# Eight of the 22 up-projection steps as seven block products, with weight sums made by adding transfers in a hybrid SSD, attention and ConvFFN layer

## The chip, the cores and the metric

The kernel runs on one core of one Trainium2 chip. A core has five engines that work side by side: TensorE (PE; its weight loads are listed as PEld), VectorE (DVE), ScalarE (ACT), GpSimd (POOL) and SyncE (SP), which here only issues transfers. Each engine has its own in-order queue and waits on semaphores; transfers (DMAs) run on 16 DMA engines. The metric is device microseconds of the whole program, as the median of several runs.

## The reference, cut to what matters

One diffusion layer over 512 latent tokens with 256 context tokens, D_MODEL = 1024, all in fp32. An input projection feeds two mixers (a bidirectional state-space scan and windowed attention); their merged output is added to x; then comes the gated ConvFFN, which is what the change is about:

```python
D_FF = 2816
def conv_ffn(h, w_up, conv_w, conv_b, w_down):
    u = dwconv_centred(h @ w_up, conv_w, conv_b)      # (512, 5632), 3 taps along the tokens
    a, b = u[..., :D_FF], u[..., D_FF:]
    return (jax.nn.silu(a) * b) @ w_down
...
x = x + gt2 * conv_ffn(modulate(x, norm2_g[l], sh2, sc2), w_up[l], ffn_conv_w[l], ffn_conv_b[l], w_down[l])
```

## The kernel before

**Products.** Every fp32 operand of a large product is split into a high part, its value rounded to fp32r, and a low part, the rest. `gemm` then issues three TensorE products for each block of 128 input channels: high weight by high input, high weight by low input, low weight by high input. The split of a weight is a ScalarE copy (the cast, `whi`) and a VectorE subtraction (`wlo`); `load` issues the transfer on SP's queue into one of three `raw` buffers and emits both. `run` goes through a list of steps; each names the weights it needs, and the next one is loaded and split one key ahead. Outside blocks marked as manual, a scheduler orders the instructions of each engine ahead of time, by its own estimate of when each is ready and by the order of the program; inside `manual_schedule` the order on the named engines is the written one.

**Attention.** A planner (`Plan`) writes out the order of the attention blocks and of 30 projections beside them (`BESIDE`, numbered g). Behind each of their weight splits (`low`, L1112), `sum_step` puts one or two transfers on POOL's queue: sums of blocks of the down projection's weight, made in DRAM. Each sum is a plain copy and then a transfer with `accum_op=ALU.add` onto it. 32 such transfers are issued here, the last behind split g = 23. The down projection already runs as seven products of blocks instead of eight (Strassen and Winograd's scheme) with them.

**The scan.** Its first group's x blocks are turned by VectorE in blocks of 32 and go out to `xs_d` and back in by transfers on POOL's queue (`blocks_out` and `blocks_in`, L1473 and L1482); VectorE weighs what came back (`xw`, L1590), and TensorE forms the states from that (L1621).

**Up projection.** 22 steps (`up_step(t)`, t = 0 to 21). Each multiplies two weights of 1024 by 128 channels, `("up", t)` for a and `("up", 22 + t)` for b, with the normed input (`h2h`, `h2l`, in the trace mh and ml): 8 blocks of k, three products each, 512 tokens wide, into two PSUM banks. Then the three taps (`conv`: one ScalarE instruction, L2058, two VectorE ones, L2059 and L2060), SiLU of a (L2066) and a times b (L2072) into `F["x"]`. After each step `f_sums(t)` works on that step's 256-column halves: sums and splits for the down projection (L2039 to L2052), six VectorE instructions for two steps. Step 0 runs in halves of 256 tokens because the norm (`norm2_k`, L2021 to L2028) only then delivers its input.

Woven between the up steps stand the last eight steps of the modulation (`m_step(24)` to `(31)`, L811 and L813, whose results go through a chain of transfers on POOL, `fold`), eight `x1_turn` (a VectorE transpose of a block of x1 into a `te` buffer, L2120, and four transfers to DRAM on SP's queue), `x1_rows` and `row_tiles`. The small buffers have tags: `te` and `tc` have two each, `ta` three, `tm` one.

Names in the trace: tile `wraw` is a weight as loaded, `whi` and `wlo` its two parts, `dsum` a sum of down weights in DRAM, `x_d` x1 in DRAM.

## Time and profile before

| | |
|---|---|
| Median of 3 runs | 1214.62 us (1214.22 to 1214.86) |
| The profiled execution | 1214.44 us |
| Its span in the trace | 1212.7 us |
| TensorE busy | 1204.0 us, 99% of the span, 6429 products |
| VectorE, ScalarE, POOL busy | 917.3, 684.6, 265.6 us |
| Up projection | from 859 us to 1101 us after the span's start |

The span runs from the first instruction recorded to the end of the last; the execution's own time has 1.7 us around it. Busy shares are means over stages that have different limits. The views used below: the page (busy times, the chain of work that ended last), busy times by stretch, groups of instructions by line and shape (busy time, mean duration in ns, idle time before), rows of single instructions in order of time (start, duration), and transfers by line (median time from issue to landing).

### The profile page before, as it was taken

The page shows a single profiled execution, that of the slowest core. Times are in us where ns is not written, and L with a number is a line of the kernel's source. Part 1 is how long each engine was busy: PE and PEld are TensorE (multiplying, and loading weights), DVE is VectorE, ACT ScalarE, POOL GpSimd, SP SyncE. Part 2 cuts the span into 40 slices and gives each one's busy share as a digit, 9 for nine tenths or more (in the row PEclk, how much of TensorE's full clock was granted, in tenths as well). Part 3 has the DMA queues.
Part 4 walks back from the last instruction along what each step waited for, and adds up shares of the span by engine and source line. Part 5 has one row for each costly group of instructions (what it writes and reads, how often), then busy time and mean ns, then how long its engine had stood idle before and what let it go on. Part 6 is the DMA issues. An engine that isn't in the chain of part 4 may idle for free.

```text
span 1212.7 us, 17847 instructions
## 1 busy us (share of the span) xinstructions
PE 1204.0 (99%) x6429; PEld 1006.4 (83%) x6429; DVE 917.3 (76%) x1476; ACT 684.6 (56%) x1269; POOL 265.6 (22%) x274
## 2 busy tenths in 40 slices
PE   9999999999999999999999999999999999999998
PEld 6798888888878878788787888888988888888886
DVE  5857887888565588788887977677677777668787
ACT  4657887778543457476575674223544343436654
POOL 0000121100102546265382780000200100110021
PEclk9999999999999999999999999999999999999999
DMA  9655789844747736567467568677265634436652
GB/s 368 257 144 185 161 232 269 169 136 137 170 153 228 229 106 197 162 161 189 147 175 265 178 232 267 223 251 236 53 163 146 200 113 139 130 106 225 213 186 97
DMA packets 129417, 224.30 MB, mean 185 GB/s; under 512 B 27336, under 2 KB 70640, under 8 KB 129328
## 3 DMA queue, kind: packets, MB, share of 16 engines
q1 hardware_dynamic: 115248, 195.61, 51.5%
q0 software_dynamic: 13792, 27.27, 10.0%
q8 instruction: 51, 0.84, 0.3%
q14 instruction: 38, 0.31, 0.1%
q10 hardware_dynamic: 288, 0.27, 0.1%
HBM read 196.17 MB, written 45.02 MB: 199 GB/s over the span
## 4 chain that ended last, share of the span: by engine, by line
PE 93%; DMA 2%; DVE 1%; POOL 1%; issue 1%; ACT 1%; DVEq 0%; POOLq 0%; ACTq 0%
PE acc L238 18%; PE acc L241 18%; PE acc L239 18%; PE score L979 3%; PE po L1028 3%; PE pt L1015 2%; PE mis L582 2%; PE mis L1759 2%; PE mis L1602 2%; DMA xs_d<-xb 2%; PE mis L2310 2%; PE mis L2311 2%; PE mis L2309 2%; PE mis L1767 1%; PE acc L2310 1%; PE acc L2311 1%
## 5 line engine op out<-in xcount | busy, mean ns | idle before, releaser
L184 DVE TENSOR_TENSOR wlo<-wraw,whi 128x1024 fp32r<-128x1024 f32 (+1 forms) x115 | 148.3, 1289 | 87.9 <-ACT whi L183 84.7
L183 ACT CAST whi<-wraw 128x1024 fp32r<-128x1024 f32 (+1 forms) x115 | 120.3, 1047 | 154.0 <-PE acc L239 104.6
L238 PE MATMUL acc<-hlh,whi 128*128 128x512 f32 x472 | 192.8, 409 | 0.0
L241 PE MATMUL acc<-hlh,wlo 128*128 128x512 f32 x472 | 185.6, 393 | 0.0
L239 PE MATMUL acc<-hll,whi 128*128 128x512 f32 x472 | 185.0, 392 | 0.0
L238 PE MATMUL acc<-mh,whi 128*128 128x512 f32 x368 | 143.3, 389 | 0.0
L239 PE MATMUL acc<-ml,whi 128*128 128x512 f32 x368 | 143.2, 389 | 0.0
L241 PE MATMUL acc<-mh,wlo 128*128 128x512 f32 x368 | 143.2, 389 | 0.0
L241 PEld LDWEIGHTS acc<-hlh,wlo 128*128 128x128 f32 x472 | 88.6, 188 | 19.9 <-issue 0.5
L238 PEld LDWEIGHTS acc<-hlh,whi 128*128 128x128 f32 x472 | 88.8, 188 | 17.6 <-issue 2.8
L239 PEld LDWEIGHTS acc<-hll,whi 128*128 128x128 f32 x472 | 88.9, 188 | 17.4 <-issue 2.2
L241 PEld LDWEIGHTS acc<-mh,wlo 128*128 128x128 f32 x368 | 69.1, 188 | 14.4
L239 PEld LDWEIGHTS acc<-ml,whi 128*128 128x128 f32 x368 | 69.1, 188 | 14.3
L238 PEld LDWEIGHTS acc<-mh,whi 128*128 128x128 f32 x368 | 69.1, 188 | 14.2
L164 POOL DMA_DIRECT2D dsum<-wdn x24 | 25.3, 1119 | 194.4 <-DVE wlo L1112 183.7
L988 DVE CUSTOM_DVE_ANT_0 p<-score,winm,nsink 128x512 f32<-128x512 f32 (+1 forms) x64 | 51.9, 810 | 15.3 <-PE score L979 13.8
L995 ACT ACTIVATE p<-p,mneg 128x512 f32<-128x512 f32 (+1 forms) x64 | 49.8, 778 | 15.4 <-DVE mneg L988 14.8
L813 DVE SCALAR_TENSOR_TENSOR tm<-wraw,csil,tm 128x512 f32<-128x512 f32 x56 | 45.8, 818 | 12.2 <-DMA wraw<-wm 11.4
L1023 DVE TENSOR_TENSOR ptl<-pt,pth 128x512 fp32r<-128x512 f32 x72 | 47.5, 686 | 8.5 <-ACT pth L1019 7.7
L238 PE MATMUL acc<-hch,whi 128*128 128x256 f32 x176 | 53.2, 302 | 0.0
L1112 DVE TENSOR_TENSOR wlo<-wraw,whi 128x1024 fp32r<-128x1024 f32 x30 | 36.7, 1223 | 18.3 <-ACT whi L1109 18.0
L241 PE MATMUL acc<-hch,wlo 128*128 128x256 f32 x176 | 49.8, 283 | 0.0
(458 smaller groups left out, 3056.9 us busy)
## 6 DMA issues: line engine op xcount, KB each, us to landing
wraw<-wup SPq DMA_DIRECT2D x44, 512.0 KB, 3.9
dsum<-wdn POOLq DMA_DIRECT2D x24, 704.0 KB, 8.5
wraw<-wm SPq DMA_DIRECT2D x32, 512.0 KB, 4.2
fb<-cs_d SPq DMA_DIRECT2D x32, 512.0 KB, 7.1
wraw<-wx SPq DMA_DIRECT2D x24, 512.0 KB, 4.1
wm<-wm SPq DMA_DIRECT2D x16, 512.0 KB, 8.3
wraw<-wz SPq DMA_DIRECT2D x16, 512.0 KB, 5.0
far<-us_d SPq DMA_DIRECT2D x32, 256.0 KB, 5.3
```

Of the source, the lines that this page charges most:

```text
L183: F["cast"] = S.copy(hi[:, :n], r[:, :n])
L184: F["sub"] = V.tensor_tensor(lo[:, :n], r[:, :n], raw(hi[:, :n]), ALU.subtract)
L238: T.matmul(ps, wh, xh[:, k0 + k, :], start=a, stop=False)
L239: T.matmul(ps, wh, xl[:, k0 + k, :], start=False, stop=False)
L241: T.matmul(ps, wl, xh[:, k0 + k, :], start=False, stop=b)
L813: V.scalar_tensor_tensor(acc, r[:, u * 512 : u * 512 + 512], sc, acc, ALU.mult, ALU.add)
L979: T.matmul(ps[:, o : o + len(z) * P], Q[h][:, b * P : (b + 1) * P], k[:, j, z[0] * P : (z[-1] + 1) * P], start=v == 0 and o % 512 in (0, P ...
L988: V.tensor_tensor_reduce(p[:, :w], d["ps"][i][:, o0 : o0 + w], m, op0=ALU.add, op1=ALU.min, scale=1.0, scalar=nsink[:, h : h + 1], accum_o ...
L995: S.activation(p, p, AF.Exp, bias=d["mneg"][:, i : i + 1], scale=-1.0, accum_out=d["den"][:, i : i + 1])
L1023: V.tensor_tensor(d["ptl"][x], d["pt"][x], raw(d["pth"][x]), ALU.subtract)
L1028: T.matmul(d["po"], vst[:, cols[x], j, :], d[y][x], start=x == 0 and y == "pth", stop=x == c - 1 and y == "ptl")
L1112: sum_step(V.tensor_tensor(d["w"][1], d["r"], raw(d["w"][0]), ALU.subtract), 1 + (4 <= g < 12))
```

## The change

**Up steps 5 to 12 as seven products.** For these eight t the 2 by 2 block matrix of weights (a and b, each in two halves of k) and the 2 by 2 block matrix of inputs (halves of k, halves of the tokens) are multiplied with seven block products instead of eight. A block product (`seven(t, j)`) is 4 blocks of k, three products each, 256 tokens wide. It needs sums of weight blocks, sums of input blocks, and additions of the products.

- *Weight sums.* For each pair of steps four sums are made in DRAM (`US`), each by a copy and an adding transfer on POOL's queue: 32 transfers more, after the 32 of the down projection. `sum_step` now issues 1 behind splits g < 4, 2 behind g = 4 to 11, and 3 from g = 12 on. The steps load them (`us`, `u4`, `ul`), beside a's own weight (`ur`).
- *Input sums.* `input_sums` behind step 0 (six VectorE instructions of 1024 elements), `input_split` behind steps 1 and 2 (four casts and four subtractions).
- *The steps.* `seven_step(t)` writes out the order of TensorE, VectorE, ScalarE and POOL. Products 7 and 4 of a step run in the next one; quarters of the result are put together from two PSUM banks and a copy kept in a `te` buffer; taps read from SBUF; a times b moves to POOL (`put_up`). `seven_in(5)` splits the first weights behind step 4; `seven_out(13)` is up step 13 with the last two products of step 12 in it.
- *The rest.* `f_sums` runs in batches of two pairs of steps behind steps 14 to 21 and no longer after each step. `x1_turn` is kept in program order: 0 to 3 behind steps 1 to 3, 4 to 7 behind every second seven-product step. One modulation step follows each of steps 0 to 3, the last four come in steps 14 to 17.

```diff
+    SEVEN = range(5, 13)
+    US = [dpool.tile([len(SEVEN), P, 1024], F32, name="usum%d" % i) for i in range(2)]
+    for i in range(0, len(SEVEN), 2):
+        wa, wb = (wup[o + SEVEN[i] : o + SEVEN[i] + 2] for o in (0, NFF))
+        s, lo, hi = slice(i, i + 2), slice(0, 512), slice(512, 1024)
+        one, two, three, four = (u[s, :, z] for u, z in ((US[0], lo), (US[0], hi), (US[1], lo), (US[1], hi)))
+        for o, first_, more in (
+            (one, wb[:, :, lo], wb[:, :, hi]), (two, one, wa[:, :, lo]),
+            (three, wa[:, :, lo], wb[:, :, lo]), (four, two, wa[:, :, hi]),
+        ):
+            SUMS += [(o, first_, {}), (o, more, dict(accum_op=ALU.add, max_dma_last_dim=512))]
...
-            sum_step(V.tensor_tensor(d["w"][1], d["r"], raw(d["w"][0]), ALU.subtract), 1 + (4 <= g < 12))
+            sum_step(V.tensor_tensor(d["w"][1], d["r"], raw(d["w"][0]), ALU.subtract), 1 if g < 4 else 2 if g < 12 else 3)
...
+    def f_sums(p0, p1, pool=False):
+        x, y = F["x"]
+        z = slice(p0, p1)
+        e, f, g, h = (a[:, z, q] for a in (x, y) for q in HALF)
+        W = G if pool else V
+        f_split(0, z, e)
+        W.tensor_tensor(e, e, f, ALU.subtract)
+        f_split(1, z, e)
+        W.tensor_tensor(f, h, f, ALU.subtract)
+        V.scalar_tensor_tensor(e, e, -1.0, h, ALU.mult, ALU.subtract)
+        V.scalar_tensor_tensor(F["t"][:, z, :], e, -1.0, g, ALU.mult, ALU.subtract)
...
+    def input_sums():
+        r = F["h2"]
+        for k in (slice(0, HK, 2), slice(HK, KT, 2)):
+            V.tensor_tensor(r[:, k, :], raw(h2h[:, k, :]), raw(h2l[:, k, :]), ALU.add)
+        b11, b12, b21, b22 = (r[:, HK * i : HK * i + HK, z] for i in range(2) for z in HALF)
+        V.tensor_tensor(b11, b11, b12, ALU.subtract)
+        V.tensor_tensor(b12, b22, b12, ALU.subtract)
+        V.scalar_tensor_tensor(b22, b11, -1.0, b22, ALU.mult, ALU.subtract)
+        V.scalar_tensor_tensor(b21, b22, -1.0, b21, ALU.mult, ALU.subtract)
+        F["four"] = b11, b22, b12, b21
...
+    def seven(t, j):
...
+        for k in range(HK):
+            wh, wl = (x[:, k * P : k * P + P] for x in w)
+            st, en = k == 0 and j in (1, 2, 5), k == HK - 1 and j in (2, 3, 4)
+            T.matmul(ps[:, :HL], wh, of(0, k), start=st, stop=False, skip_group_check=True)
+            T.matmul(ps[:, :HL], wh, of(1, k), start=False, stop=False, skip_group_check=True)
+            T.matmul(ps[:, :HL], wl, of(0, k), start=False, stop=en, skip_group_check=True)
...
+    def put_up(t):
+        G.tensor_tensor(F["x"][t % 2][:, t // 2, :], B["oa", t], B["ob", t], ALU.mult)
...
+    def seven_step(t):
+        n, a, b = t + 1, t - 1, t - 2
...
+            with tc.manual_schedule(engines=EVERY):
+                if old:
+                    quarter(a, 12)
+                seven(t, 5)
+                if new:
+                    sum_cast("us", n)
+                if older:
+                    conv_rest("b", b, NFF + b)
+                    put_up(b)
+                if old:
+                    conv_first("a", a, a, "tb")
+                kept_half(t, 0, B["y", t])
+                if new:
+                    sum_low("us", n)
+                seven(t, 1)
+                if new:
+                    whole_cast(n)
+                kept_half(t, 1, B["x", t])
+                if old:
+                    conv_rest("a", a, a)
+                    seven(a, 7)
+                if new:
+                    sum_cast("u4", n)
+                sum_cast("ul", t)
+                if old:
+                    quarter(a, 22)
+                if new:
+                    whole_low(n)
+                if old:
+                    silu_a(a)
+                seven(t, 2)
+                quarter(t, 11)
+                if new:
+                    sum_low("u4", n)
+                sum_low("ul", t)
+                seven(t, 3)
+                quarter(t, 3)
+                if old:
+                    seven(a, 4)
+                    quarter(a, 21)
+                    conv_first("b", a, NFF + a, "tm")
+                seven(t, 6)
...
-            V.transpose(t, x1[c // 4][:, c % 4, :])
+            tc.keep_in_program_order(V.transpose(t, x1[c // 4][:, c % 4, :]))
...
+        + [up_step(0), ([], input_sums)] + msteps[24:25] + [up_step(1), ([], lambda: (input_split(0), input_split(1)))]
+        + msteps[25:26] + [x1_turn(0), up_step(2), ([], lambda: (input_split(2), input_split(3)))]
+        + msteps[26:27] + [x1_turn(1), up_step(3), x1_turn(2), x1_turn(3)] + msteps[27:28] + [up_step(4), seven_in(SEVEN[0])]
+        + weave([seven_step(t) for t in SEVEN], [x1_turn(c) for c in range(4, 8)]) + [seven_out(SEVEN[-1] + 1)]
         + weave(
-            weave([up_step(t) for t in range(18)], msteps[24:]) + [up_step(t) for t in range(18, NFF)],
-            [([], lambda: None)] * 6 + [x1_turn(c) for c in range(8)] + [x1_rows] + [([], lambda: None)] * 6 + [([], row_tiles)],
+            [up_step(t) for t in range(SEVEN[-1] + 2, 18)],
+            [([], lambda: f_sums(0, 2)), ([], lambda: f_sums(2, 4))] + msteps[28:] + [x1_rows],
+        )
+        + weave(
+            [up_step(t) for t in range(18, NFF)],
+            [([], lambda p=p: f_sums(p, min(p + 2, DK))) for p in (4, 6, 8, 10)] + [([], row_tiles)],
         )
```

More of the change, by code (lines that the diff above doesn't have):

```diff
@@ new lines, in input_split, with sum_cast, sum_low @@
+    def input_split(i):
+        x = F["four"][i]
+        hi, lo = (F["T"][:, v, i, :].rearrange("p (k n) -> p k n", k=HK) for v in range(2))
+        S.copy(hi, x)
+        V.tensor_tensor(lo, x, raw(hi), ALU.subtract)
+    B = {}
+    RING = {"us": "sring", "ul": "lring", "u4": "oring"}
+    def sum_cast(key, t):
+        hi, _ = B[key, t] = F[RING[key]][t % 2]
+        r = B["raw" + key, t]
+        S.copy(hi, r[:, 0:512] if key == "u4" else r)
+    def sum_low(key, t):
+        hi, lo = B[key, t]
+        r = B["raw" + key, t]
+        V.tensor_tensor(lo, r[:, 0:512] if key == "u4" else r, raw(hi), ALU.subtract)
@@ new lines, in seven_step, with fn @@
+    def seven_step(t):
+        n, a, b = t + 1, t - 1, t - 2
+        new, old, older = n in SEVEN, a in SEVEN, b in SEVEN
+        keys = [(key, n) for key in NEXT if new] + [("ul", t)]
+        def fn(*w):
+            for (key, i), r in zip(keys, w):
+                B["raw" + key, i] = r
+            with tc.manual_schedule(engines=EVERY):
[40 more added lines that the diff above has]
+                seven(t, 6)
+        return keys, fn
@@ new lines, in seven_out, with fn @@
+    def seven_out(t):
+        a, b = t - 1, t - 2
+        def fn(wa, wb):
+            quarter(a, 12)
+            conv_rest("b", b, NFF + b)
+            conv_first("a", a, a, "tb")
+            conv_rest("a", a, a)
+            silu_a(a)
+            pa, pb = accb(), accb()
+            with tc.manual_schedule(engines={mybir.EngineType.PE}):
+                gemm([(pa, h2h, h2l)], wa, ks=range(0, 4))
+                seven(a, 7)
+                quarter(a, 22)
+                gemm([(pa, h2h, h2l)], wa, ks=range(4, 8))
+                seven(a, 4)
+                quarter(a, 21)
+            put_up(b)
+            conv_first("b", a, NFF + a, "tm")
+            conv_rest("b", a, NFF + a)
+            put_up(a)
+            th = up_first(pa, pb, t)
+            gemm([(pb, h2h, h2l)], wb)
+            up_second(th, pb, t)
+            open_ends()
+        return [("up", t), ("up", NFF + t)], fn
```

127 lines of the change are left out of this document (105 added, 22 removed).

## The prediction

> **What bounds the kernel now.** I read the page's first part and the chain first, then the up projection's stretches, then TensorE's rows.
>
> ```profile
> span 1212.7 us, 17847 instructions
> ...
> PE 1204.0 (99%) x6429; PEld 1006.4 (83%) x6429; DVE 917.3 (76%) x1476; ACT 684.6 (56%) x1269; POOL 265.6 (22%) x274
> ...
> PE 93%; DMA 2%; DVE 1%; POOL 1%; issue 1%; ACT 1%; DVEq 0%; POOLq 0%; ACTq 0%
> ```
>
> TensorE is busy 99% of the span and carries 93% of the chain that ended last. So whatever removes TensorE work from a dense stretch shortens the run, and whatever lets another engine be late there lengthens it. The busy times by stretch (step 0, steps 1 to 4, the first step's end, steps 5 to 12, steps 13 to 20; steps counted at the pace found below) show how much room the others have:
>
> ```profile
> core 0: us, PE busy (x) PEld busy (x) DVE busy (x) ACT busy (x) POOL busy (x), PEclk, DMA share, GB/s
> 859.00:873.00 14.00, 13.87 (x111) 13.20 (x110) 11.17 (x23) 9.02 (x20) 5.53 (x8) 1.00 0.40 76
> 873.00:916.50 43.50, 43.50 (x194) 36.10 (x195) 33.79 (x50) 19.02 (x26) 0.00 (x0) 1.00 0.56 140
> 875.00:886.00 11.00, 11.00 (x50) 9.10 (x49) 9.59 (x15) 6.02 (x9) 0.00 (x0) 1.00 0.50 127
> 916.50:1004.00 87.50, 87.50 (x387) 72.47 (x386) 62.55 (x89) 35.64 (x49) 7.09 (x9) 1.00 0.51 155
> 1004.00:1101.00 97.00, 97.00 (x429) 80.36 (x428) 67.06 (x98) 40.12 (x55) 7.05 (x9) 1.00 0.38 119
> ```
>
> TensorE has no hole in the up projection; VectorE is busy 71 to 87%, ScalarE about 40%. The two rates that decide the gain come from TensorE's rows: 512-column products of an up step, 135 rows of which the first and last stand here, and the 256-column ones of the last output steps, 36 rows:
>
> ```profile
> 904.50 0.39 PE L238 MATMUL acc<-mh,whi 128*128 128x512 f32 x1
> ...
> 934.87 0.39 PE L241 MATMUL acc<-mh,wlo 128*128 128x512 f32 x1
> ```
>
> ```profile
> 840.72 0.28 PE L1943 MATMUL acc<-mh,wlast 128*128 128x256 f32 x1
> ...
> 844.92 0.28 PE L1942 MATMUL acc<-ml,wlast 128*128 128x256 f32 x1
> ```
>
> Start to start that is 30.37/134 = 0.2266 us for 512 columns and 4.20/35 = 0.120 us for 256. Half the columns cost 53%, not half.
>
> **The change, part by part.**
>
> *Seven products for eight.* An up step is 2 x 8 x 3 = 48 products of 512 columns, 48 x 0.2266 = 10.88 us. A seven-product step is 7 x 4 x 3 = 84 products of 256 columns, 84 x 0.120 = 10.08 us. Eight steps: 8 x 0.80 = 6.4 us gained. The arithmetic saved is 12.5%, the time only 7.3%. Two blocks of the last such step run inside step 13; they are counted in the 84.
>
> *VectorE and ScalarE inside those steps.* Durations of like instructions:
>
> ```profile
> L184 DVE TENSOR_TENSOR wlo<-wraw,whi 128x1024 fp32r<-128x1024 f32 x40 | 49.0, 1225 | 54.2 <-ACT whi L183 53.5 <-DMA x_d<-te 0.7
> L183 ACT CAST whi<-wraw 128x1024 fp32r<-128x1024 f32 x40 | 42.2, 1056 | 53.3 <-PE acc L239 53.1
> L2060 DVE SCALAR_TENSOR_TENSOR ta<-acc,vec,ta 128x511 f32<-128x511 f32 x21 | 15.7, 747 | 0.5
> L2058 ACT ACTIVATE ta<-acc,vec 128x512 f32<-128x512 f32 x20 | 15.5, 774 | 0.0
> L2072 DVE TENSOR_TENSOR fx<-tb,tc 128x512 f32<-128x512 f32 x20 | 13.8, 692 | 0.7
> L2066 ACT ACTIVATE tb<-ta 128x512 f32<-128x512 f32 x20 | 12.7, 634 | 46.8 <-DVE ta L2060 44.6 <-DVE g2c L2144 2.2
> L813 DVE SCALAR_TENSOR_TENSOR tm<-wraw,csil,tm 128x512 f32<-128x512 f32 x14 | 10.5, 750 | 0.9 <-DMA wraw<-wm 0.6
> L2039 DVE TENSOR_TENSOR fs<-fx,fs 128x256 fp32r<-128x256 f32 x22 | 9.2, 420 | 4.3 <-ACT fs L2038 4.3
> L2120 DVE STREAM_TRANSPOSE te<-x 128x512 f32<-128x512 f32 x5 | 3.5, 704 | 0.0
> ```
>
> ```profile
> L1955 ACT ACTIVATE tc<-x 128x256 f32<-128x256 f32 x4 | 1.7, 418 | 5.9 <-DVE x L2013 5.2 <-DVE a L1922 0.6
> ```
>
> VectorE, per step: three low parts of 1024 (3.68), one of 512 (0.69), four taps (3.0), three quarter sums at 0.42 (1.26): 8.6 us, and 0.70 more after every second step for a transpose: 9.3 of 10.08. ScalarE: three casts (3.17), one of 512 (about 0.63), two taps (1.55), SiLU (0.63), four quarter copies (0.42 each, 1.7): 7.7. Both orders are written out, so what counts is when each is late: the first quarter sum releases product 7, 2.9 us later in TensorE's order; the subtraction after product 7 releases product 4, 2.9 us later again; the next step's weights are split at least 3 us ahead. I cost this at nothing; the cover is these slacks. A step's loads on SP's queue grow from 1.05 to 1.84 MB, 182 GB/s, where the stretch now moves 155 at a share of 0.51; a buffer is free at least 6 us before its next split: nothing.
>
> *Transposes that share a buffer.* The transposes of x1 now come in order between these steps and take one of two `te` buffers, which the kept quarters need too. One of its transfers lands so long after its issue (median, us):
>
> ```profile
> x_d<-te SPq DMA_DIRECT2D x32, 64.0 KB, 3.8
> ```
>
> A transpose ends about 9.4 us into a step, its four transfers leave within about 2 us and land 3.8 us later, 5 us into the next step; the kept quarter wants the buffer at 1.9 us and TensorE waits for it at product 3, 5.8 us in. It fits by 0.4 us. Bounds: 0 to 3 us for each of three such places; I take 0.2 each, 0.6.
>
> *Input sums in steps 0 to 4.* Six VectorE instructions of 1024 elements come in at once behind step 0, 6 x 1.225 = 7.35 us, and step 24 of the modulation comes ahead of the next split (two instructions of at most 0.75, 1.5). The place where this is paid is the split of step 1's second weight:
>
> ```profile
> 876.73 1.22 DVE L184 TENSOR_TENSOR wlo<-wraw,whi 128x1024 fp32r<-128x1024 f32 x1
> ...
> 877.86 0.69 DVE L2072 TENSOR_TENSOR fx<-tb,tc 128x512 f32<-128x512 f32 x1
> ...
> 878.66 0.39 PE L238 MATMUL acc<-mh,whi 128*128 128x512 f32 x1
> ...
> 879.11 0.39 PE L241 MATMUL acc<-mh,wlo 128*128 128x512 f32 x1
> ```
>
> That split ends at 877.95 and TensorE uses it at 879.11: 1.2 us of slack. Until 876.73 VectorE has idle 2.8 us (14.00 - 11.17) in step 0, about 1 us after, and three transposes of 0.70 go elsewhere: 5.9 us of room for 8.85. So it comes 2.95 us later, 1.8 us too late. From the other side: VectorE's work until step 5 was 11.17 + 33.79 = 45.0 us; eight transposes leave (5.6), four come back (2.8), the sums for the down projection leave (12 x 0.42 = 5.0), input sums (7.35) and their four splits (4.9) come, the modulation adds two steps (about 3), the first seven-product weights 0.7: 53.1 us. At 87%, the fullest that VectorE is in these steps (9.59 of 11), that takes 61 us and not 57.5: 3.5 late. Bounds 0 (the splits slip in front) and 3.5; I take 2.0.
>
> *Sums for the down projection, in batches.* Eleven pairs at six instructions of 0.69 for two pairs, 22.7 us, in steps 14 to 21: 2.8 us a step on top of 2 x 1.225 + 4 x 0.747 + 0.69 = 6.1, with the modulation's last four steps 1.5 more in half of them: 10.4 of 10.88 at worst. Nothing, covered by that 0.5 us and by the four steps without modulation.
>
> *Weight sums by adding transfers.* 32 more transfers on POOL's queue, behind splits 16 to 26 of the attention. Weight loads there are issued three splits ahead; TensorE stayed dense while the DMA share was 0.98,
>
> ```profile
> 180.00:210.00 30.00, 30.00 (x166) 25.58 (x165) 23.88 (x51) 23.10 (x45) 5.13 (x7) 1.00 0.98 275
> ```
>
> so slower loads cost nothing. The cost can only come through POOL's order, which the slow rival takes up; here 0.
>
> **Sum.** -6.4 + 0.6 + 2.0 = -3.8 us. The profiled execution took 1214.44 us (its span and 1.74 around it), 0.18 under the median 1214.62: 1214.44 - 3.8 = 1210.6.
>
> **The rivals.**
>
> *Everything is hidden.* If the splits go ahead of the input sums: 1214.4 - 6.4 = 1208.0, the floor. The 1.2 us of slack speaks against it.
>
> *VectorE binds, no change.* Price: 3.5 us at the start, and in the seven-product steps the 0.8 us won each. For it speaks the pair
>
> ```profile
> 863.96 0.73 POOL L2026 TENSOR_TENSOR ml<-ta,mh 128x256 fp32r<-128x256 f32 x1 [0.97 <-ACT ta L2025]
> 863.98 0.99 DVE L2028 SCALAR_TENSOR_TENSOR ml<-tb,mod,mh 128x256 fp32r<-128x256 f32 x1
> ```
>
> ```profile
> L2028 DVE SCALAR_TENSOR_TENSOR ml<-tb,mod,mh x8: 441/484/994, 856.0 to 871.2; 128x256 fp32r<-128x256 f32 x8
> ```
>
> ```profile
> L1579 POOL TENSOR_TENSOR st<-st,eT 128x512 f32<-128x512 f32 x24 | 29.3, 1223 | 56.2 <-ACT st L1623 38.3 <-DVE st L1605 17.9
> ```
>
> where a VectorE instruction with two SBUF inputs that follows a POOL one ends 0.28 us after it and takes twice the 0.48 us usual on its line. The product of a and b moves to POOL in all eight steps, and one of this size takes POOL about 1.22 us. If it held VectorE for 0.5 (as in this pair) to 1.2 us each time, 8.6 or 9.3 becomes 9.1 to 10.5, around 10.08. Against it: starts follow each other sooner than durations say (877.86 behind the 1.22 us begun at 876.73), some 0.08 us for each of eleven. Price: 3.5 + 8 x 0.3 on top of -6.4 + 0.6: 1214.5. [...]
>
> *POOL is late for the x blocks, slower.* New sums come as copy, then add onto the same rows, so each add waits on POOL for its copy to land, and everything behind it on POOL waits too. Single transfers landed (column: us) in 8.1 for an add and 5.1 for a copy of 704 KB:
>
> ```profile
> dsum<-wdn POOLq DMA_DIRECT2D x1, 704.0 KB, 8.1
> ```
>
> ```profile
> dsum<-dsum POOLq DMA_DIRECT2D x1, 704.0 KB, 5.1
> ```
>
> ```profile
> 246.10 0.58 POOL L164 DMA_DIRECT2D dsum<-dsum  x1 [8.22 <-DVE wlo L1112]
> ...
> 325.93 1.24 POOL L164 DMA_DIRECT2D dsum<-wdn  x1 [11.24 <-DVE wlo L1112]
> 378.20 4.96 POOL L1473 DMA_DIRECT2D xs_d<-xb  x8 [51.03 <-DVE xb L1464]
> ...
> 392.15 5.02 POOL L1473 DMA_DIRECT2D xs_d<-xb  x8 [3.56 <-DVE xb L1464]
> ```
>
> ```profile
> 429.40 3.70 PE L1621 MATMUL mis<-xw,Bkc 128*128 128x512 f32 x8 [0.98 <-DVE xw L1590]
> ```
>
> The new ones start at split 16 (246 us). 512 KB at 5 and 8 us, one after another, take 16 x 13 = 208 us: 454. With the independent ones overlapping, about 42 us for each group of eight: 414. If POOL's order fills the waits, they end some 26 us behind split 26 (338): 365. POOL is needed at 378 for the first group's x blocks, which can slip 8 us for free, because the second set waits for VectorE until 392; from there each microsecond is one of TensorE's at 429, where it waits 0.98 us already. So at 386 + 3.8 = 390 the gain is gone, and at 414 it costs 28 us, less what is caught up. Times 1217 to 1238, middle 1222. In this ordering nothing in the trace excludes it, which is why it has over a quarter. [...]
>
> **How the numbers follow.** A measurement of this kernel tells 0.2%, 2.4 us, from no change. Forecast (1209.2 to 1212.2) 0.40, hidden 0.12, VectorE binds (1212.2 to 1217) 0.21, POOL late 0.27. Faster: 0.38 of the forecast, and 0.12: 0.50. Same: 0.21 and 0.02 = 0.23. Slower: 0.27. Range: from 1208.0, the floor, to 1225, which leaves out about half of the POOL case. The point is the forecast's 1210.6, own range 1209.2 to 1212.2.
>
> **What would show it.** Seven-product steps 10.1 us apart, 256-column starts 0.120 us apart; a TensorE hole of 1 to 3 us near 879 behind a low part that waited for input sums; none inside steps 5 to 12 beyond 0.5 us. The last weight sum issued on POOL before the x blocks and before 390. Wrong if TensorE's first states come much later than 429, if POOL's product stretches VectorE's low parts beyond 1.3 us, or if holes recur each step.

## The result: slower by 3.7%, and the profile after

| | before | after |
|---|---|---|
| median of the runs, us | 1214.59 (1214.22 to 1214.86, 4 runs) | 1260.36 (1256.70 to 1262.10, 4 runs) |
| ratio | | 1.0373, 95% interval 1.0350 to 1.0396 |
| first states product starts, us | 429.4 | 475.2 |
| first product of the ssd output | 721.1 | 760.4 |
| last product of the output weights | 858.99 | 899.16 |
| first product of the down projection | 1101.72 | 1147.27 |

1210.6 was forecast, and the range ended at 1225. The landmarks place the loss. 45.8 us are lost ahead of the first states product. 6.5 us of them come back by the ssd output, since TensorE did projections in the meantime (it is 60 to 70% busy in the hole). The up projection (the last two rows) takes 248.1 us in place of 242.7, where it was to be 3.8 us shorter. The down projection takes as long as before, within 0.5 us.

The page after, first part, slices, chain and POOL's queue (before: TensorE 99%, chain 93% TensorE, 13792 packets and 27.27 MB on this queue):

```profile
PE 1212.3 (96%) x6717; PEld 1021.7 (81%) x6717; DVE 946.7 (75%) x1488; ACT 708.4 (56%) x1311; POOL 320.2 (25%) x314
...
PE   9999999999999668999999999999989999999997
...
PEclk9999999999999878999999999999989999999999
...
q0 software_dynamic: 32736, 44.05, 17.7%
...
PE 73%; issue 12%; DMA 5%; DVE 5%; POOL 2%; ACT 1%; SPq 0%; DVEq 0%; POOLq 0%; ACTq 0%
```

A slice is a fortieth of the span of 1258.7 us, 31.5 us. The hole lies mostly in the 14th and 15th, 409 to 472 us, with a lower clock in and behind it (8, 7 and 8 tenths in the 14th to 16th). The chain now has 12% of issue and 5% of DMA, 1% and 2% before. The end of the weight sums on POOL after, then all of them grouped, then the first states product:

```profile
405.21 2.37 POOL L175 DMA_DIRECT2D usum<-wup  x2 [12.57 <-issue]
421.77 0.60 POOL L175 DMA_DIRECT2D usum<-usum  x1 [14.19 <-DVE wlo L209]
424.33 1.84 POOL L175 DMA_DIRECT2D usum<-wup  x1 [1.96 <-DMA usum<-wup]
434.25 1.77 POOL L175 DMA_DIRECT2D usum<-wup  x1 [8.08 <-issue]
435.28 2.75 POOL L1502 DMA_DIRECT2D xs_d<-xb  x3
```

```profile
L175 POOL DMA_DIRECT2D usum<-wup x24: 600/1775/1845, 248.4 to 434.2; - x24
...
  issue: 61.2, 7
  DMA usum<-wup: 46.1, 8
...
DMA to landing us min/median/max: 4.0/9.6/17.7
```

```profile
L1650 PE MATMUL mis<-xw,Bkc x6: 1061/1061/1223, 475.2 to 479.6; 128*128 128x512 f32 x6
```

The last sum leaves POOL at 434.25, and the first x block, due at 378, goes out right behind it at 435.28. POOL stood 46.1 us for landings and 61.2 us for nothing that the profile names. This is the rival "POOL is late for the x blocks", with a later end than its 414.

In the up projection, the hole that was forecast near 879 stands 47 us later, at 926. TensorE and VectorE there, and the stretch by clock:

```profile
922.76 0.40 PE L268 MATMUL acc<-ml,whi 128*128 128x512 f32 x1
926.36 0.79 PE L270 MATMUL acc<-mh,wlo 128*128 128x512 f32 x1 [3.20 <-DVE wlo L209]
926.95 0.63 PE L267 MATMUL acc<-mh,whi 128*128 128x512 f32 x1
927.38 0.63 PE L268 MATMUL acc<-ml,whi 128*128 128x512 f32 x1
```

```profile
923.96 1.21 DVE L2164 SCALAR_TENSOR_TENSOR h2raw<-h2raw 128x1024 f32<-128x1024 f32 x1
925.09 1.21 DVE L209 TENSOR_TENSOR wlo<-wraw,whi 128x1024 fp32r<-128x1024 f32 x1
```

```profile
921.00:932.00 11.00, 7.23 (x20) 5.04 (x20) 11.00 (x12) 5.11 (x7) 0.00 (x0) 0.69 0.17 48
```

The input sums (h2raw) run ahead of the weight's low part (wlo), as feared, and TensorE waits 3.20 us. Behind the hole products start 0.43 us apart, not 0.2266, at a granted clock of 0.69 over these 11 us. A hole of this length is not needed for that: in step 0 of after a hole of 1.28 us and a few small products have slow ones behind them (0.213 us between starts of 256 columns from 904 to 907, a granted clock of 0.79 from 902 to 910), and e1 (the run without the sums, below) has a hole of 1.44 us there and a clock of 0.76 from 859 to 873, while behind a like hole in e16 (1.3 us of waiting) the clock is 1.00 (860 to 870). What decides it, no run shows.

In every second seven-product step a third, shorter hole returns:

```profile
988.88 0.28 PE L2220 MATMUL mis<-mh,wlo 128*128 128x256 f32 x1
989.79 0.39 PE L2218 MATMUL mis<-mh,ringrbc 128*128 128x256 f32 x1 [0.63 <-ACT te L2225]
```

The next two such holes end at 1010.84 and 1031.87. So two steps take 21.04 us with one hole of 0.79 in them, that is 10.13 us a step without it.

### The profile page after: what moved, and what is told of

The parts are those of the page before. It is cut to its first block, busy times and chain, and to the rows that moved or that the text cites. A ratio compares the mean times of both kernels' runs of the same rounds, so it can differ in the third digit from the quotient of the medians.

```text
span 1258.7 us, 18593 instructions
## 1 busy us (share of the span) xinstructions
PE 1212.3 (96%) x6717; PEld 1021.7 (81%) x6717; DVE 946.7 (75%) x1488; ACT 708.4 (56%) x1311; POOL 320.2 (25%) x314
## 3 DMA queue, kind: packets, MB, share of 16 engines
q0 software_dynamic: 32736, 44.05, 17.7%
## 4 chain that ended last, share of the span: by engine, by line
PE 73%; issue 12%; DMA 5%; DVE 5%; POOL 2%; ACT 1%; SPq 0%; DVEq 0%; POOLq 0%; ACTq 0%
PE acc L267 12%; PE acc L270 12%; PE acc L268 12%; PE score L1008 3%; PE po L1057 3%; PE pt L1044 2%; PE mis L611 2%; PE mis L1788 2%; PE mis L1631 2%; PE mis L2548 2%; PE mis L2547 2%; PE mis L2546 2%; PE mis L1796 1%; PE acc L2548 1%; PE acc L2547 1%
## 5 line engine op out<-in xcount | busy, mean ns | idle before, releaser
L208 ACT CAST whi<-wraw 128x1024 fp32r<-128x1024 f32 (+1 forms) x99 | 103.3, 1045 | 147.7 <-PE acc L268 82.3
L209 DVE TENSOR_TENSOR wlo<-wraw,whi 128x1024 fp32r<-128x1024 f32 (+1 forms) x99 | 129.6, 1309 | 74.4 <-ACT whi L208 73.9
L267 PEld LDWEIGHTS acc<-hlh,whi 128*128 128x128 f32 x472 | 89.2, 189 | 17.7 <-issue 2.8
L270 PE MATMUL acc<-mh,wlo 128*128 128x512 f32 x240 | 94.3, 394 | 3.2 <-DVE wlo L209 3.2
L267 PE MATMUL acc<-mh,whi 128*128 128x512 f32 x240 | 94.6, 394 | 0.6 <-DVE ta L2104 0.6
L268 PE MATMUL acc<-ml,whi 128*128 128x512 f32 x240 | 94.2, 392 | 0.0
L175 POOL DMA_DIRECT2D usum<-wup x24 | 35.6, 1620 | 112.9 <-issue 61.2
L1459 ACT ACTIVATE tb<-ta 128x512 f32<-128x512 f32 (+1 forms) x44 | 23.3, 532 | 68.9 <-DVE ta L1453 50.1
L270 PEld LDWEIGHTS acc<-mh,wlo 128*128 128x128 f32 x240 | 45.6, 190 | 13.3 <-DVE wlo L209 3.6
L267 PEld LDWEIGHTS acc<-mh,whi 128*128 128x128 f32 x240 | 45.6, 190 | 10.7 <-ACT whi L208 1.0
L1753 ACT ACTIVATE E<-fb,TX 128x128 f32<-128x128 f32 x128 | 44.3, 389 | 16.4 <-DMA fb<-cs_d 8.7
```

The source lines that it names most:

```text
L175: dma = G.dma_start(o, x, **how)
L208: F["cast"] = S.copy(hi[:, :n], r[:, :n])
L209: F["sub"] = V.tensor_tensor(lo[:, :n], r[:, :n], raw(hi[:, :n]), ALU.subtract)
L267: T.matmul(ps, wh, xh[:, k0 + k, :], start=a, stop=False)
L268: T.matmul(ps, wh, xl[:, k0 + k, :], start=False, stop=False)
L270: T.matmul(ps, wl, xh[:, k0 + k, :], start=False, stop=b)
```

## The experiments

Eighteen kernels, of which e8, e12, e15 and e18 were timed in four runs and the others in one; the kernel before ran beside each of them (medians 1214.4 to 1214.9). In the expectations, "the run before" is e5 for e6, e6 for e7, e7 for e8 and e11 for e12. "Up" is the time from the last product of the output weights to the first of the down projection. In the changed code it is 246.4 to 249.7 us from run to run; between 246.4 and 246.7 in six of the profiles. The four runs of after span 5.4 us and those of e12 4.1, so the times of single runs that lie less than about 5 us apart do not settle which is faster; there the landmarks and waits of the profiles have to, and each of these is one execution.

| run | edit against | time, us | first states | up |
|---|---|---|---|---|
| before | | 1214.6 | 429.4 | 242.7 |
| after | | 1260.4 | 475.2 | 248.1 |
| e1 | after, no sums | 1221.4 | 428.9 | 249.7 |
| e2 | after, interleaved | 1250.1 | 465.6 | 246.7 |
| e3 | after, x blocks on SP | 1257.6 | 447.6 | 248.2 |
| e4 | after, large pieces | 1236.7 | 453.5 | 246.4 |
| e5 | e2 and e4 together | 1235.9 | 452.8 | 246.7 |
| e9 | e1 with two sums | 1230.2 | 446.2 | 246.6 |
| e10 | after, rows and columns | 1283.7 | 493.0 | 246.7 |
| e11 | e5 and e10 together | 1224.9 | 436.0 | 246.7 |
| e13 | e11, sums earlier | 1222.9 | 430.9 | 247.4 |
| e6 | e5's sums at 720 to 865 us | 1279.0 | 429.7 | 248.1 |
| e7 | e6, input sums spread | 1276.1 | 429.6 | 248.3 |
| e8 | e7, turns moved, small buffer | 1271.5 | 430.1 | 243.1 |
| e12 | e11 with e8's three edits | 1221.8 | 434.5 | 242.8 |
| e14 | e12, modulation later | 1257.4 | 439.9 | 273.0 |
| e15 | e14, sums earlier | 1250.9 | 430.6 | 275.9 |
| e16 | e13, turns moved | 1217.2 | 429.1 | 243.8 |
| e17 | e13, input sums spread | 1225.7 | 430.3 | 247.1 |
| e18 | e13, three edits, POOL | 1223.3 | 430.3 | 250.4 |

**What the sums cost at all (e1).**

```diff
-            SUMS += [(o, first_, {}), (o, more, dict(accum_op=ALU.add, max_dma_last_dim=512))]
+            pass
-        nc.sync.dma_start(r, US[0][t - SEVEN[0]])
+        nc.sync.dma_start(r, wup[t])
```

> The 32 new transfers are left out, and the seven-product steps load the plain up weights in place of the sums, so the weight sums are missing from what is computed; everything behind the loads is as in the changed kernel. Every theory that puts the loss into the attention's transfers (order on POOL, the queue's rate, contention) expects the first states product back at 429 us (429.40 before, 475.18 after) and, since the up projection stays as it is, a time of 1214.4 + 6.4 = about 1221 us: the changed kernel is 39.1 us behind when the last output weights are used and 45.5 us behind at its end, so 6.4 us are lost in the up projection. If the loss came from the up projection's seven products or from the loads of the sums, the time would stay above 1250.

Measured 1221.39, states at 428.87. So the 32 transfers cost 39.0 us, all of them ahead of the states, and the up projection the other 7.0 (249.72 - 242.73).

**What holds POOL (e2, e4, e5).** e2 orders the list by rank over the four groups, so three transfers lie between a copy and its add (not four, as the expectation has it); e4 only changes the piece.

```diff
+    SUMS += [RANK[4 * i + j][k] for j in range(4) for k in range(2) for i in range(4)]
...
-            (o, more, dict(accum_op=ALU.add, max_dma_last_dim=512))
+            (o, more, dict(accum_op=ALU.add, max_dma_last_dim=2048))
```

> All 32 transfers stay, in another order: the four groups of eight are interleaved, so four transfers lie between a copy and the add onto its rows. Theory A (POOL stands waiting for each copy to land before it may issue the add): those waits go, the 32 issues of 1.6 us each take 51 us behind their splits, the last one leaves POOL before 378, the first states come at 429 to 432 and the time is 1221 to 1224. Theory B (the queue or the memory moves these bytes at its own rate, whatever the order): the last sum still leaves at 420 to 434 and the time stays at 1245 to 1260.

> The sums keep their order; the adding transfers of the up weights move pieces of 2048 bytes in place of 512, so a quarter of the packets. If the landing time of an add (7.2 to 16 us) is made of its 1024 small packets, adds land in 4 to 8 us, the last sum leaves POOL near 434 - 16 x 5 = 354 to 390 and the time is 1221 to 1230. If an add's time is that of its bytes or of a fixed latency, the last sum still leaves at 425 to 434 and the time stays at 1250 to 1260.

> The interleaved order and the pieces of 2048 bytes together, sums still in the attention. Theory A2 (two separate waits hold POOL: in the old order an add waits for its copy to land; an add of 1024 pieces also isn't issued until the add before it has landed, as the interleaved run showed with issues 8 to 14 us apart behind no semaphore): now neither is left, each transfer is issued in 0.6 to 1.3 us, the last one leaves POOL within 5 us of split 26, before 350, the x blocks go out at 378 to 386, and what is left is what the traffic costs the splits: 1222 to 1232 us. Theory B (the bytes set the pace): the last sum leaves at 370 or later and the time is 1236 or more, as with the large pieces alone.

e2: 1250.1, with the last sum at 425.44: the numbers of theory B, but by luck, since e4 and e5 move the same bytes sooner. POOL between 299 and 338 us, four adds that wait for nothing that a semaphore shows:

```profile
300.37 1.83 POOL L177 DMA_DIRECT2D usum<-wup  x1 [1.01 <-DVE mneg L1019]
311.94 1.79 POOL L177 DMA_DIRECT2D usum<-wup  x1 [9.73 <-issue]
321.67 1.75 POOL L177 DMA_DIRECT2D usum<-wup  x1 [7.95 <-issue]
332.23 4.06 POOL L177 DMA_DIRECT2D usum<-wup  x5 [8.80 <-issue]
```

Each add is issued about as the one before it lands (the first three land 11.2, 9.4 and 10.2 us after their start), while the last row takes an add and four copies of 256 pieces in a row without a wait. So a second wait holds POOL: an add in 1024 pieces keeps the next one out. e4 removes that one, with the landing waits left (POOL's waits of e4):

```profile
POOL usum L175 <- DMA usum<-wup: 53.0, 13, 8.7
POOL xs_d L1502 <- DVE xb L1493: 37.8, 4, 19.4
POOL usum L175 <- DMA usum<-usum: 26.5, 7, 8.0
...
POOL usum L175 <- issue: 3.1, 1, 3.1
```

"issue" falls from 61.2 us (after) to 3.1, the last sum leaves at 376, and 23.6 us are won: the first theory by the last sum, though the time is 6.7 us above its range. e5 has neither wait and its last sum leaves at 355, later than the 350 that I had put, and yet it is no faster than e4 and 3.9 us above its range. In both POOL now waits for VectorE (19.4 us before one x block): something else is late.

**The order on VectorE (e9, e10, e11).** VectorE of e5, where the third x block stands behind two weight splits; before, it was at 401.9:

```profile
420.47 1.23 DVE L211 TENSOR_TENSOR wlo<-wraw,whi 128x1024 fp32r<-128x1024 f32 x1 [1.48 <-ACT whi L210]
425.84 1.23 DVE L211 TENSOR_TENSOR wlo<-wraw,whi 128x1024 fp32r<-128x1024 f32 x1 [4.14 <-ACT whi L210]
426.98 0.70 DVE L1495 STREAM_TRANSPOSE xb<-tc 128x512 f32<-128x512 f32 x1
```

The order of instructions on an engine is fixed when the program is built. after, e2, e4 and e5 share this one; e1 has that of before. e9 keeps only the first two sums, which is enough to get this order; e10 only describes each transfer in another way, which is enough to lose it; e11 joins e10 with e5.

```diff
+    del SUMS[34:]        # e9: the 32 sums of the down weights and two more
...
+            fl = lambda v: v.rearrange("a p c -> (a p) c")
+            (fl(o), fl(first_), {}), (fl(o), fl(more), dict(accum_op=ALU.add, max_dma_last_dim=512))
```

> Of the 32 transfers only the first copy and the first add are kept (1 MB in all, issued at 247 us), and the loads take the plain up weights as in the run with none, so the weight sums are missing from what is computed. With these two the program that is built has VectorE's instructions in another order: the third pair of x-block transposes, at 402 us before, stands behind two weight splits that ran at 421 and 426 us in the runs with all sums. Theory D (that order costs by itself): first states near 453 as in the two runs with large pieces, 1234 to 1237 us, with POOL free from 262 on. Theory A (only POOL's waits and the traffic cost): first states at 429, 1221.4 us.

> The changed kernel with one edit: each of the 32 transfers is described by rows and columns (256 x 512) in place of slabs, rows and columns (2 x 128 x 512); the bytes, their order and the pieces are the same. The program built from it has VectorE's order of the kernel before up to the up projection. POOL's waits are still there. If those waits set the time alone, the last sum still leaves POOL near 434 and the time is 1250 to 1260; if the order was all of it, 1222. The order was worth 1235.9 - 1221.4 = 14.5 us where POOL was free, and less should come back here, since x blocks that go out at 435 are late for either order.

> All 32 sums in the attention, interleaved, in pieces of 2048 bytes, and described by rows and columns, so that VectorE's order is that of the kernel before. POOL's waits and the order are both gone; what is left is the traffic. Theory: first states at 429 to 433 and 1221.4 to 1225 us, nearly that of the run without sums. If the traffic itself holds up the splits (a modulation load took 9.15 us to land at 368 with the large pieces), 1226 to 1230.

e9: 1230.24, with POOL free since 262 us: the order alone costs 8.9 us (states at 446, of which the stages after it regain half). The 14.5 expected were too many. e11: 1224.9, as expected (its states come at 436.0, 3 us later than I had put), 11.0 below e5 by the order; POOL's sums stand alike in both (last one at 353.74 and 355.38). e10 missed on the other side: 1283.7, 23 us slower than after. Its VectorE and what TensorE waited for:

```profile
461.34 0.71 DVE L1494 STREAM_TRANSPOSE xb<-tc 128x512 f32<-128x512 f32 x1 [44.83 <-DMA xs_d<-xb]
```

```profile
PE acc L268 <- DVE ta L1454: 48.4, 2, 47.4
```

With the old order, the third x block comes early on VectorE and needs the buffer of the first, which POOL had not yet sent; VectorE stands 44.83 us, and TensorE with it. But e10 does not change VectorE's order alone. POOL's sums too are built in another order than in after, against what the expectation says: POOL stands 124.6 us for landings in place of 55.9 (15.1 us of "issue" in place of 61.2), and its end comes 17 us later:

```profile
451.08 1.76 POOL L176 DMA_DIRECT2D usum<-wup  x1 [7.96 <-DMA usum<-usum]
452.09 2.75 POOL L1503 DMA_DIRECT2D xs_d<-xb  x3
```

The states follow the first x block by 40.9 us in e10 and by 39.9 in after. So 17 of the 23 us go with POOL's later end; the other 6 are lost between the states and the ssd output, probably because less work had passed in the meantime. What VectorE's order alone is worth while POOL is late, no run shows. Once POOL is not late, the new order costs 9 us (e9) to 11 us (e11).

**Where the traffic goes (e3, e6, e13).** e3 issues the x blocks on SP's queue, e6 puts the interleaved, large-piece sums behind the splits of the ssd-output and output weights, e13 has e11's sums at three per split from split 4 to 23.

```diff
-                G.dma_start(o, t[32 * a : 32 * a + 32, :]...            # e3
+                nc.sync.dma_start(o, t[32 * a : 32 * a + 32, :]...
...
+        if key[0] in ("os", "out"):                                     # e6
+            LATE and sum_step(sub, 2, LATE)
...
+            sum_step(..., 1 if g < 4 else 3 if g < 24 else 0)           # e13
```

> The sums stay as they are, and the transfers of the first group's x blocks (out and back) are issued by SP's queue in place of POOL's. Theory A (everything behind the sums waits on POOL): the x blocks go out at 378 as before, the first states come at 429 to 436 and the time is 1221 to 1228; the sums go on to 434 beside them. Theory C (the sums' traffic slows the x blocks and the weights of this stage): the x blocks take much longer than before to land (over 10 us in place of 4 to 5), the states come at 450 or later, and the time is above 1240.

> The same 32 transfers as in the run before (interleaved, large pieces), but behind the splits of the ssd-output and output weights (720 to 860 us), where POOL has little else; the attention is that of before. If the place in the attention is the whole cost, the first states come at 429 and the time is that of the run without sums, 1221.4 (1220.5 to 1223). If the sums cost their traffic wherever they stand, or the one small POOL operation of that stretch (the root at 778) is held up by them, TensorE has a new hole there and the time is 1224 to 1235.

> As the run with all waits and the order mended (1224.9), but with three transfers behind each split from split 4 to split 23, so that the last sum leaves POOL near 315 in place of 354 and none is under way at 368, where TensorE stood 4.9 us for a cast behind a slow modulation load. If the remaining 3.5 us are this late traffic, 1221.0 to 1222.5; if the traffic costs as much wherever it stands in the attention, 1224 to 1226.

e3: 1257.6, states at 447.6: the time of theory C without its mechanism, since the first x blocks land in 3.2 to 8.1 us. They go out at 384.6, but the loads of the x weights now stand behind them on SP, and TensorE waits 12.1 us for a cast at 437; another 19 us went between 448 and 758, which I did not follow up. The wait changed its queue. e6: 1279.0, far above both cases expected: states at 429.7, then TensorE has holes from 727 on. What TensorE waited for from 720 to 865 us:

```profile
PE acc L272 <- ACT yh L1881: 12.1, 1, 12.1
PE acc L272 <- ACT whi L213: 11.0, 4, 6.0
PE acc L275 <- DVE wlo L214: 9.7, 5, 4.9
```

The weights of this stretch (`wos`) land in 6.5 us (5.3 before), beside sums that land in 9.8, and their splits are late; the three rows are 32.8 us of the 57.6 that e6 lies above e1, and the rest I have not worked out (the granted clock is 0.87 from 720 to 865). The attention hides the same bytes almost wholly. e13: 1222.9 and no wait for a cast at 370, where e11 has one of 4.7 us; so late sums in the attention cost about 2 us by the time. The rest of the traffic costs 1.5 us by the time, and 3.9 by the last product of the output weights (862.78 against 858.92 in e1).

**The up projection (e7, e8, e12, e14 to e18).** Three edits: the input sums spread (additions behind step 1, the rest behind step 2, splits behind steps 3 and 4); x1's last four transposes in steps 14 to 17; the first half of step 0's scratch in `ta` again.

```diff
+            t = F["h2"][:, k, z] if u else tmp("ta")[:, :HL]
...
-        + weave([seven_step(t) for t in SEVEN], [x1_turn(c) for c in range(4, 8)])
+        + [seven_step(t) for t in SEVEN]
...
-        + [up_step(0), ([], input_sums)] + msteps[24:25] + [up_step(1), ([], lambda: (input_split(0), ...
+        + [up_step(0)] + msteps[24:25] + [up_step(1), ([], lambda: input_sums(0))]
```

> As the run before, and the input sums spread: the two additions behind step 1, the rest behind step 2, their splits behind steps 3 and 4, in place of all six behind step 0. If the hole of 3.4 us before step 1's second weight is VectorE doing input sums ahead of that weight's low part, then the hole and the 0.2 us that each of the products after it takes longer go: 7.3 us (4.21 + 1.63 + 1.30 + 0.12 us above the usual spacing in the run without sums), so 1214 (1213 to 1216). If VectorE has no room in steps 1 to 4 at all, the hole moves to a later step and the time stays within 2 us of 1221.

> As the run before, and two more edits: the four transposes of x1 stand in steps 14 to 17 in place of the seven-product steps, and the first half of step 0's scratch goes to the small buffer again in place of the h2 buffer. If the three holes of 0.79 us come from the shared buffer te and step 0's hole of 1.44 us from ScalarE waiting for the h2 buffer's memory, which the last output products still read, another 2.4 and 3.4 us go: 1214.4 - 6.4 + 0 to 2 = 1208 to 1210, the floor of the seven products. If the up projection has another limit (VectorE in steps 13 to 17, which now get four transposes), 1211 to 1215.

> The run before plus the three edits of the up projection: input sums spread over steps 1 to 4, x1's last four transposes in steps 14 to 17, the first half of step 0's scratch in the small buffer. If the three holes (7.3, 2.4 and 3.4 us) go, the time is that of the run before less 9 to 13 us: 1208 to 1213, below the kernel before (1214.4). If VectorE has no room elsewhere for what was moved, 1214 to 1219.

> The run with early sums (1222.9) and one edit: x1's last four transposes stand in steps 14 to 17 and not between the seven-product steps. If they hold the buffer te that the kept quarters need, the three holes of 0.79 us go: 2.4 us less, 1220.5 (1220 to 1221). If something else makes these holes, 1222.9.

> The run with early sums (1222.9) and one edit: the input sums spread over steps 1 to 4. If VectorE has no room in these steps (it was busy 21.5 of 22 us with this order), the hole of 3.4 us at step 1 goes and others of the same sum come at steps 2 to 5: 1220 to 1223. If it has room, 7 us less: 1216.

e7 (1276.1) and e8 (1271.5, ratio 1.0442 to 1.0477) stand on e6 and tell only by their "up": 248.3 and 243.1. e16: 1217.2; TensorE's waits of e13 hold a row `PE mis L2221 <- ACT te L2228: 1.9, 3, 0.6` that e16 has not, all three holes are gone, and up is 3.6 us shorter (the other 2.1 of the 5.7 lie ahead of the up projection). So the turns that the transposes take of the buffer make these holes; how, is told below. e17: 1225.7; the hole of 3.4 is gone and others are there (2.8 at 925, 0.7, 0.5), up is 247.1 against 247.4: nothing won. The 2.8 us on the time lie ahead of the up projection (a hole of 3.2 at 858 behind a POOL root) and are left open. e12: 1221.8 (1219.59 to 1223.72, ratio 1.0052 to 1.0086), 3.2 below e11's single run and not 9 to 13. Its VectorE in steps 1 and 2 has no room:

```profile
880.00:902.00 22.00, 20.87 (x94) 16.59 (x93) 21.52 (x27) 12.40 (x16) 0.00 (x0) 1.00 0.47 132
```

Two ways to give it room:

```diff
-        + [up_step(0)] + msteps[24:25] + [up_step(1), ...               # e14, e15: msteps[24:28] in steps 14 to 17
+        + [up_step(0), up_step(1), ...
...
-                V.tensor_tensor(r[:, k, :], raw(h2h[:, k, :]), raw(h2l[:, k, :]), ALU.add)
+                G.tensor_tensor(r[:, k, :], raw(h2h[:, k, :]), raw(h2l[:, k, :]), ALU.add)   # e18
```

> As the run with the three edits of the up projection (1221.8, the profiled one 1219.6), and the four modulation steps that stood in steps 1 to 4 now stand in steps 14 to 17. That takes 8 VectorE instructions of 0.75 us, 6 us of the 52 in steps 1 to 4. If VectorE's room is the limit there (busy 21.5 of 22 us), the holes at 885, 916 and 918 us and the slow products behind them (9.2 us above the usual spacing, of which some 2 us are step 0's own) mostly go: 1214 to 1217. If the order of the input sums itself makes the holes, 1219 to 1222.

> Both edits together: the early sums and the emptied steps 1 to 4. If each does what is expected of it, 1214.4 - 6.4 + 2 to 5 = 1210 to 1213, below the kernel before. If neither does, 1220 to 1224.

> The run with early sums and all three edits of the up projection, and the four additions and subtractions of two operands in the input sums (and the half one that the small buffer needs) on POOL. VectorE loses 5 to 6 us of work in steps 1 to 4. If its room is the limit there, the holes at 885 to 920 (7 us with the slow products behind them) mostly go: 1219.8 - 5 = 1213 to 1216. If a POOL instruction holds VectorE's instructions up for its length (2.4 us each on 1024 columns), nothing is won: 1219 to 1222.

e14: 1257.4, e15: 1250.9 (1.0277 to 1.0311). The modulation's last steps feed a row that the down projection needs, through transfers on POOL one behind another, and that row came late (TensorE's waits of e14):

```profile
PE mis L2391 <- DVE g2c L2389: 23.1, 1, 23.1
PE acc L270 <- ACT whi L211: 6.9, 1, 6.9
```

Up to 1077 us the time above the usual spacing fell from 9.1 us (e12) to 7.0 (e14): room on VectorE explains a part; what the rest is stays open. e18: 1223.3 (1.0048 to 1.0082), up 250.4. With the additions on POOL, TensorE waits 2.1 us for POOL in step 0 and 3.5 us for a tap on VectorE behind it, so nothing was won. No version beat the kernel before. The nearest, e16, is 0.2% above it in one run: its sums cost nothing that shows at the states (429.1), the eight steps gain their 6.4 us, and the hole of the input sums and step 0 take 7.5 us of it back (243.8 - 242.7 + 6.4).

## Why the prediction was wrong, step by step

**"Weight sums by adding transfers ... here 0" is the step that failed, by 39.0 us (e1).** The trace told enough. The working under the POOL rival had the two facts, in-order waits on POOL and a need at 378, and priced their end at 414 or 454; 434.25 was measured, between them. Its own rule, that each microsecond beyond 386 is one of TensorE's at the states, gives 434.25 - 386 = 48, and 45.8 were lost there, 39.3 after the catching up by the ssd output. e10 bears the rule out once more: 451.08 - 386 = 65, and 63.6 were lost at its states. I gave this case 0.27 because POOL's order might fill the waits. The list of transfers left little to fill them with: each group was written as copy, add, copy, add, and only the third of its four sums does not start from the one before it. It should have been the forecast. Three of its parts were not seen: the pieces of 512 bytes keep a second add out (e2 against e5; 61.2 us of "issue"), adds of that form took 7.2 to 16.0 us to land (median 9.5) where 8.1 us for 704 KB was taken, and the program's order on VectorE and on POOL changes with the transfers (e9, e10). That the end lies between the two prices is therefore partly luck.

**Seven products for eight, -6.4: right.** 10.13 us a step without the buffer's hole, against 10.08.

**x1 transposes and `te`, +0.6: right place, a quarter of the size, and another mechanism.** Three holes of 0.79, 2.4 us; 3.6 us of the up projection by e16. The working let the transpose's own transfers hold the buffer until they land. They land in 2.2 to 4.6 us here, the last at 986.05 for the hole that ends at 989.79, and ScalarE copies the next quarter 3.3 us later. What it waits for is the rows below (after, cut to VectorE, POOL and ScalarE):

```profile
985.30 1.22 DVE L2185 TENSOR_TENSOR ringa<-sraw,ringa 128x1024 fp32r<-128x1024 f32 x1
985.54 2.12 POOL L2255 TENSOR_TENSOR fx<-tb,tm 128x512 f32<-128x512 f32 x1 [7.68 <-DVE tm L2249]
986.43 1.78 DVE L2248 SCALAR_TENSOR_TENSOR tb<-ta,vec,tb 128x511 f32<-128x511 f32 x1
...
988.91 0.41 DVE L2238 SCALAR_TENSOR_TENSOR tc<-te,acc 128x256 f32<-128x256 f32 x1
989.36 0.37 ACT L2225 COPY te<-mis 128x256 f32<-128x256 f32 x1 [4.28 <-DVE tc L2238]
```

`te` has two buffers. Where a transpose takes one, the next kept quarter gets the one of the step before, and that is read until VectorE's quarter sum (`tc`) ends. This sum is late because the tap before it (`tb`, L2248) takes 1.78 us beside the product on POOL, and 0.75 where none runs (975.46). By these rows, an estimate, the sum would end a microsecond earlier without the product beside the tap, and the hole of 0.79 would not be there; no run tries that.

**Input sums, +2.0: the hole was 3.4 us, in the place named** and at the upper bound of 3.5. What was missing is the lower clock behind it: with the products at 0.43 us the place costs about 7 us (the spacing above the usual in e1: 4.21 + 1.63 + 1.30 + 0.12). The second bound, VectorE at its fullest, was the better one: e17 and e12 show that moving the sums only moves the hole.

**Step 0 was left out of the sum.** The scratch that moved from `ta` to the h2 buffer is written 3.8 us later there. ScalarE before, then in e1, whose output stage ends within 0.1 us of before's:

```profile
856.24 0.50 ACT L2025 ACTIVATE ta<-tb,mod 128x256 f32<-128x256 f32 x1
```

```profile
860.08 0.89 ACT L2054 ACTIVATE h2raw<-tb,mod 128x256 f32<-128x256 f32 x2
```

The likely reason is that this memory belongs to the output stage until its last product at 858.92. TensorE has a hole of 1.44 us at 861 and slow products behind it; e12, with `ta` again among its edits, has 0.45 us there. Of the 5.4 us that the up projection of after takes longer, about 2 are left for this step, an estimate: -6.0 for the eight steps, 2.4 for the three holes, 6.8 at the input sums.

**VectorE binds** did not come true in the seven-product steps (69 of 84 us busy) but did in steps 1 to 4. The slowing that it was priced on is there all the same, in the rows above: POOL's product, begun beside a low part of VectorE, takes 2.12 us (1.22 was taken), the low part keeps its 1.22 us, and the tap that comes next on VectorE takes 1.78 in place of 0.75. So VectorE loses about 1.0 us in six of the eight steps, within the 0.5 to 1.2 that the rival put, and has room for it except where a buffer waits. **Sums for the down projection in batches, 0: right**; TensorE was busy throughout 1053 to 1147 us.

## What to carry to other kernels

Transfers on one queue that depended on each other, copy and then add onto the same rows, were a chain of landing times here (4.0 to 17.7 us each, 46.1 us of POOL's waits in after); lay out such a chain against the moment when the queue is next needed, and take its slow end as the forecast unless the list itself breaks the chain. Put independent transfers between the dependent ones and use large pieces: here the first alone brought 10 us, the second alone 24. When transfers are added, compare the built order of instructions on every engine, the issuing one included, since here it moved the critical work by 8.9 us (e9) with POOL free.

## What the hardware showed that I had not expected

An adding transfer of 512 KB in pieces of 512 bytes was issued only when the one before it had about landed (in e2 starts lie 9.7 to 11.6 us apart, and an add lands 9.4 to 11.2 us after its start), though no semaphore was waited for; in pieces of 2048 bytes the same transfer was issued in about 0.9 us and a following one at once (e5). A TensorE hole of 3.4 us cost 2 to 3 us more, by ten (after) to fourteen (e1) products at 0.43 us. The same 32 transfers cost 1.5 us of time beyond e1 in the attention (e13) and 57.6 us at 720 to 865 us (1279.0 - 1221.4), with the DMA share high in both places (1.00 from 228 to 345 in e13, 0.93 from 720 to 865 in e6). And a tap on VectorE that begins while a product runs on POOL took 1.75 to 1.79 us in place of 0.75 (all six such taps of after), although the trace shows no semaphore between them; one that began 0.23 us ahead of the product kept its 0.75 (1038.35).
